# Rotary halves as separate chunks, four heads' scores in four 32-row groups, and ranked first loads

## The chip, the cores and the metric

One Trainium2 chip; the kernel runs on one of its cores. The metric is the device time of one execution in microseconds (us), the median of several runs. Engines are named as the profile names them: PE (TensorE matmul), PEld (its weight loads), DVE (VectorE), ACT (ScalarE), POOL (GpSimd), SP (SyncE, which issues most DMAs here).

## The reference

Two layers over a sequence of 256 tokens with 1024 channels, all float32. A layer first projects x to 7168 columns: a convolution branch (1024), differential attention q, k, v (512 each), a second attention q, k, v (512 each; its blocks are 256 keys long, so at this length it is plain causal attention), and 3072 gate columns. Both attentions rotate q and k before the scores; a head has 64 dimensions, and its first 32 are paired with its last 32:

```python
def apply_rope(x, cos, sin):
    x1, x2 = jnp.split(x, 2, axis=-1)
    return x * c + jnp.concatenate([-x2, x1], axis=-1) * s
```

so the rotated first half is x1·cos − x2·sin and the second x2·cos + x1·sin. Scores are q·k over the 64 dimensions, masked, softmaxed, and multiplied with v. The convolution branch is a causal depthwise convolution of 31 taps over 512 channels, then a LayerNorm. The three branches are projected, gated, summed and projected again (LayerNorm), and a squared-ReLU MLP with 4096 hidden units follows (LayerNorm).

## The kernel before

**Precision.** Every large weight and activation is split into a rounded part ("hi", by ACT) and the rest ("lo", by DVE), and a product is three matmuls (`mm3`, line 392). A weight tile is 512 KB: a DMA into one of 4 `raw` buffers, an ACT cast to `whi`, a DVE subtraction to `wlo` (`Weights.get`, line 342; 8 buffers each). Scores, the transposed probabilities and the transposes are plain fp32 matmuls, which the profile shows as two passes each.

**Order.** No instruction is issued where it is written. All are recorded in a plan (class `Plan`, line 42), and `order` (line 235) then builds one fixed list per engine: it walks forward in a clock of its own, and whenever an engine is free gives it the ready operation with the earliest latest-start time (`late`, line 181). For this clock it books a price for each operation (lines 131 to 147): for PE 0.422 ns a column with a floor of 108 ns, for a plain fp32 matmul 1.69 ns a column (so 433 ns for 256 columns and 216 ns for 128); for DVE 1.042 ns an element and 68 ns, 62 more with a per-partition scalar. The plan knows nothing of matmuls that run side by side in different rows of the array. On the chip the lists stay as they are: an engine that is early waits at its next list entry. PSUM is 8 banks in three pools, `pm` 2, `pa` 4 and `pt` 2 (line 30).

**Head.** x transposed comes in five pieces over SP, between the first weights (lines 448 to 457). The convolution's input projection of layer 0 runs over output half b, then over the eight 128-row slices kt, then over the two token tiles t (line 601), so all of x and the first four weights are needed before the second four. Weight tile i of the eight holds slices 2(i mod 4) and 2(i mod 4)+1 of output half i//4.

**Attention.** After the v projections come eight units of 128 columns x 2 (q and k of two attentions, two halves each; `qkunit`, line 566), two weights each; after each weight `tick` (line 579) runs the attention steps that are due. A unit's two column chunks are two pairs of heads, with 64 partitions to a head. `rope` (line 639) moves the halves of each head past each other by four ACT copies of 32 partitions, then multiplies twice and adds on DVE. `attn_scores` (line 657) does one pair of heads: four matmuls with 64 contraction rows, two `pa` banks. The further steps of a pair (transpose, times v, normalise, transpose back) use `pa` too and are due three ticks apart; pairs start at ticks 7, 9, 11, 14, 16, 18, 20 and 22 (line 777). Ticks 1 to 16 are the q and k weights, 17 to 24 the first gates.

**Gates.** `tunit` (line 545) makes 256 gate columns in two halves of 8 + 8 matmuls, the first half in a `pm` bank, the second in a `pt` bank; `tsum` (line 561) empties each bank by one ACT and one DVE instruction. It also serves the MLP.

**Convolution taps.** 124 DVE instructions a layer (`tap`, line 589) that only the LayerNorm in the last gates needs. They are ready all the time, so the planner fills every free moment of DVE with them.

Of the kernel before, what the change touches and what calls it, by code (L numbers as in the profile page):

```python
# [9 lines left out]
F32 = mybir.dt.float32  # L10
# [31 lines left out]
class Plan:  # L42
# [11 lines left out]
    class Op:  # L54
        __slots__ = ("i", "eng", "cost", "fn", "deps", "succ", "tiles", "late", "start", "end",
                     "bytes", "left", "ready", "bias")

# [9 lines left out]
    def __init__(self, nc):  # L67
        self.nc = nc
        self.ops = []
        self.tiles = {}  # L70
        self.tags = {}
        self.bias = 0.0
        for k, e in (("PE", nc.tensor), ("Activation", nc.scalar), ("DVE", nc.vector),
                     ("Pool", nc.gpsimd), ("SP", nc.sync)):
            setattr(self, k, Plan.Engine(self, e, k))
# [34 lines left out]
    def record(self, name, fn, method, args, kw):  # L110
# [10 lines left out]
        op.bytes = 0  # L121
        op.bias = self.bias
        op.fn = lambda: fn(*args, **kw)  # L123
        main = outs[-1] if "out" not in kw else kw["out"]
# [110 lines left out]
    def order(self):  # L235
        ops = self.ops
        self.latest()
        for op in ops:
            op.late += op.bias
            op.left = len(op.deps)  # L240
            op.ready = 0.0
            op.start = None
# [89 lines left out]
class Weights:  # L332
# [8 lines left out]

    def get(self, **dims):
        plan, i = self.plan, self.i
        self.i += 1
        raw = plan.tile(self.pool, [P, 1024], F32, "raw", RAWS)
        hi = plan.tile(self.pool, [P, 1024], F32R, "whi", NW)
        lo = plan.tile(self.pool, [P, 1024], F32R, "wlo", NW)
        n = 512 if i < 3 else 1024
        for c in range(0, 1024, n):
            s = slice(c, c + n)  # L350
            plan.SP.dma_start(raw[:, s], self.order[i][:, s])
            plan.Activation.copy(hi[:, s], raw[:, s])
            plan.DVE.tensor_sub(lo[:, s], raw[:, s], hi[:, s].bitcast(F32))
        pat = "p (" + " ".join(list(dims) + ["n"]) + ") -> p " + " ".join(list(dims) + ["n"])
        return [a.rearrange(pat, **dims) for a in (hi, lo)]
# [3 lines left out]
def kernel(ctx: ExitStack, tc: tile.TileContext, x, xT, w_in, w_p2, w_o, w_f1, w_f2,  # L359
# [52 lines left out]
    for l in range(L):  # L412
        order += [w_in[l, i] for i in range(32)]
        for step, b in GATED:
            if step == "gate":
                order += [w_in[l, 32 + 8 * b + i] for i in range(8)]
            else:
                order += [w_p2[l, 4 * b + i] for i in range(4)]
        order += [w_o[l, i] for i in range(8)]
        f1 = [w_f1[l, i] for i in range(32)]  # L420
        f2 = [w_f2[l, i] for i in range(32)]
        order += f1[:6]
        for i in range(6, 32, 2):
            order += f2[i - 6:i - 4] + f1[i:i + 2]
        order += f2[26:]
# [22 lines left out]
    X = x_new()  # L448
    for h in range(2):
        a = slot(F32, "xt32")  # L450
        for c0, c1 in ((0, 256), (256, 512), (512, 1024)) if h == 0 else ((0, 512), (512, 1024)):
            s = slice(c0, c1)
            k = (4 * h + c0 // 256) % 2
            n = (c1 - c0) // 256
            R.SP.dma_start(a[:, s], xT[:, h * 1024 + c0:h * 1024 + c1])
            split(*[v[:, k:k + n] for v in x_pair(X, 2 * h + c0 // 512)],
                  a[:, s].rearrange("p (k n) -> p k n", k=n))
    cst_t = R.tile(const, [P, 896], F32, "cst", 1)
# [62 lines left out]
    for l in range(L):  # L521
# [22 lines left out]

        def tunit(ticks=True):
            out = []
            for c in range(2):
                w = W.get(k=KT)
                ps = bank(("pm", "pt")[c])
                hi, lo = w  # L550
                for kt in range(KT):
                    R.PE.matmul(ps, hi[:, kt], x_both(X, kt), start=kt == 0, stop=False)
                for kt in range(KT):
                    R.PE.matmul(ps[:, 0:SEQ], lo[:, kt], x_at(X, kt)[0], start=False,
                                stop=kt == KT - 1)
                out.append(ps)
                if ticks:
                    tick()
            return out
# [38 lines left out]

        wc = [W.get(k=2) for _ in range(8)]
        pp = [[bank("pa"), bank("pm")] for _ in range(NT)]  # L600
        seq = [(t, b, kt) for b in range(2) for kt in range(KT) for t in range(NT)]
        if l:
            seq.sort(key=lambda e: e[0])
        for t, b, kt in seq:
# [32 lines left out]


        def rope(ps, dst):
            qq = R.tile(work, [P, 1024], F32, "zz", 3)  # L640
            q, qr = qq[:, :512], qq[:, 512:]
            for a in range(0, P, 64):
                R.Activation.copy(qr[a:a + 32], ps[a + 32:a + 64])
                R.Activation.copy(qr[a + 32:a + 64], ps[a:a + 32])
            p3 = ps.rearrange("p (c n) -> p c n", c=2)
            q3 = q.rearrange("p (c n) -> p c n", c=2)
            qr3 = qr.rearrange("p (c n) -> p c n", c=2)
            cb = cosT.rearrange("p (o n) -> p o n", o=1).broadcast_to([P, 2, SEQ])
            sb = sinT.rearrange("p (o n) -> p o n", o=1).broadcast_to([P, 2, SEQ])
            R.DVE.tensor_mul(q3, p3, cb)  # L650
            R.DVE.tensor_mul(qr3, qr3, sb)
            R.DVE.tensor_add(dst, q, qr)

        QK = {}
        o_sb = {}

        def attn_scores(b, pair):

            q, k = [QK[b, w, pair // 2][:, pair % 2] for w in 'qk']
            pt = R.tile(work, [P, 2, 384], F32, "pt", 2)  # L660
            mn = col(4, "mn")
            ll = col(4, "ll")
            li = col(4, "li")
            for e in range(2):
                ps = bank("pa")
                r = slice(64 * e, 64 * e + 64)
                R.PE.matmul(ps[:, 0:256], q[r, 128:256], k[r], start=True, stop=True)
                R.PE.matmul(ps[:, 256:384], q[r, 0:128], k[r, 0:128], start=True, stop=True)
                for (s, m, j) in ((slice(0, 256), slice(0, 256), 2 * e),
                                  (slice(256, 384), slice(128, 256), 2 * e + 1)):  # L670
                    R.DVE.tensor_tensor_reduce(
                        out=pt[:, e, s], in0=ps[:, s], in1=maskq[:, m], scale=-0.125,
                        scalar=3.0e38, op0=ALU.add, op1=ALU.min, accum_out=mn[:, j:j + 1])
                    R.Activation.activation(pt[:, e, s], pt[:, e, s], AF.Exp, bias=mn[:, j:j + 1],
                                         scale=-1.0, accum_out=ll[:, j:j + 1])
            R.DVE.reciprocal(li, ll)
            return pt, ll, li

        def transp(src):

            ps = bank("pa")
            R.PE.transpose(ps[:, 0:128], src[:, 256:384], ident)
            R.PE.transpose(ps[:, 128:256], src[:, 0:128], ident)
            R.PE.transpose(ps[:, 256:384], src[:, 128:256], ident)
            return ps
# [10 lines left out]

        def d_a(h):
            pt, ll, li = attn_scores(0, h)
            cc = col(2, "cc")
# [16 lines left out]
        def d_c(h):  # L716
            t, li = state['d', h]
            ps = bank("pa")
            hs = slice(h * 128, (h + 1) * 128)
# [17 lines left out]
        def d_d(h):  # L737
            o = state['d', h]
            ps = bank("pa")
            R.PE.transpose(ps[:, 0:128], o[:, 128:256], ident)  # L740
# [3 lines left out]

        def m_a(j):
            pt, ll, li = attn_scores(1, j)
            for e in range(2):
# [13 lines left out]
        def m_c(j):  # L761
            t = state['m', j]
            t = t.rearrange("p (e n) -> p e n", e=2)
            ps = bank("pa")
            for k, (c0, c1) in enumerate(((0, 256), (256, 384))):
# [8 lines left out]

        jobs = [[lambda f=f, h=h: f(h) for f in (d_a, d_b, d_c, d_d)] for h in range(4)]
        jobs += [[lambda f=f, h=h: f(h) for f in (m_a, m_b, m_c)] for h in range(4)]
        start = [7, 9, 11, 14, 16, 18, 20, 22]
        ev = []
        for i, (j, s) in enumerate(zip(jobs, start)):
            for k, f in enumerate(j):  # L780
                ev.append((s + 3 * k, -k, i, f))
        for e in sorted(ev, key=lambda e: e[:3]):
# [185 lines left out]
        for i in range(3, 16):  # L968
            do2(i - 3)
            ps = tunit()  # L970
            hsplit(i, ps)
# [23 lines left out]
def _layout(x, w_in, b_gate, conv_w, conv_b, conv_ln_g, conv_ln_b, w_conv_out,  # L995
# [21 lines left out]
    for l in range(L):  # L1017
# [3 lines left out]
        for q, k in ((dq, dk), (mq, mk)):  # L1021
            a, b = tu(q), tu(k)
            u += [a[:2], b[:2], a[2:], b[2:]]
# [23 lines left out]
    cosT = np.concatenate([c, c, c, c])  # L1047
    sinT = np.concatenate([-s, s, -s, s])
    i = np.arange(P)
# [28 lines left out]
```

## Time and profile before

| what | value |
|---|---|
| time, median of 3 runs | 861.02 us (860.42 to 861.96) |
| the profiled execution: its own time | 865.14 us |
| the profiled execution: its span | 861.8 us |
| PE busy, share of the span | 843.6 us, 98% |
| DVE busy | 657.2 us, 76% |
| ACT busy | 544.7 us, 63% |
| DMA, mean over the span | 182 GB/s |

The span is from the first to the last instruction of the core. Matmuls are pipelined and the ends shown are modelled, so starts of matmuls are compared rather than ends. A group's idle time is that of its engine just before it, with what ended the wait.

### The profile page before, as it was taken

The numbers are of one execution on the slowest core, as the hardware profiler recorded it, in microseconds if no ns is written. First come the engines' busy times: TensorE is split into PE (matmuls) and PEld (weight loads), VectorE is DVE, ScalarE is ACT, GpSimd is POOL, SyncE is SP. The second block draws the span as 40 slices with busy tenths as digits, with TensorE's granted clock in tenths as the row PEclk, the third lists the DMA queues.
The fourth block names the chain that finished last, engine by engine and source line by source line (L and its number), as shares of the span: only waits on it lengthen the run. The fifth ranks groups of instructions, "written<-read, shape, count | busy, mean of one in ns | idle before, by whom it ended". The sixth has DMA issues, their size and how long they took to land.

```text
span 861.8 us, 13202 instructions
## 1 busy us (share of the span) xinstructions
PE 843.6 (98%) x4938; PEld 738.3 (86%) x4938; DVE 657.2 (76%) x1124; ACT 544.7 (63%) x917; POOL 18.1 (2%) x26
## 2 busy tenths in 40 slices
PE   7999989999999999999999999999999999999996
PEld 5889978889988888888888999888898888888885
DVE  5789999997876755555688999999787876555545
ACT  6558899567437666666354789975562586666650
POOL 0000000000000000000000001000000000000000
PEclk9999999999999999999999999999999999999999
DMA  8865433556536856655355853355644577665511
GB/s 314 296 206 175 146 104 123 173 189 200 168 144 226 302 191 192 195 195 194 100 176 180 269 157 124 98 175 175 211 144 152 185 282 241 196 195 188 186 66 49
DMA packets 44559, 156.95 MB, mean 182 GB/s; under 512 B 4944, under 2 KB 5712, under 8 KB 44496
## 3 DMA queue, kind: packets, MB, share of 16 engines
q1 hardware_dynamic: 44496, 156.13, 54.7%
q8 instruction: 38, 0.62, 0.3%
q14 instruction: 25, 0.20, 0.1%
HBM read 155.06 MB, written 1.05 MB: 181 GB/s over the span
## 4 chain that ended last, share of the span: by engine, by line
PE 88%; DVE 4%; ACT 3%; DMA 3%; issue 1%; SPq 1%; POOL 0%; DVEq 0%; ACTq 0%
PE pm L123 42%; PE pa L123 30%; PE pt L123 16%; DMA raw<-in_w_f_dram 2%; DVE wlo L123 1%; DVE big L123 1%; ACT zz L123 1%; DMA big<-in_xT_dram 1%; ACT pt L123 1%; ACT o L123 1%; SPq L123 1%; ACT whi L123 0%; ACT big L123 0%; DVE pt L123 0%; DVE col L123 0%
## 5 line engine op out<-in xcount | busy, mean ns | idle before, releaser
L123 DVE TENSOR_TENSOR wlo<-raw,whi 128x1024 fp32r<-128x1024 f32 (+1 forms) x283 | 341.2, 1211 | 143.4 <-ACT whi L123 141.8
L123 ACT CAST whi<-raw 128x1024 fp32r<-128x1024 f32 (+1 forms) x283 | 293.7, 1044 | 184.9 <-PE pm L123 62.7
L123 PE MATMUL pm<-big,whi 128*128 128x256 f32 (+1 forms) x1296 | 270.2, 320 | 0.1
L123 PEld LDWEIGHTS pm<-big,whi 128*128 128x128 f32 x1296 | 215.4, 191 | 17.6 <-DVE big L123 0.7
L123 PE MATMUL pa<-whi,big 128*128 128x512 f32 x704 | 219.2, 393 | 3.4 <-ACT big L123 2.1
L123 PE MATMUL pm<-big,wlo 128*128 128x256 f32 x848 | 182.4, 282 | 0.0
L123 PEld LDWEIGHTS pa<-whi,big 128*128 128x128 f32 x704 | 130.4, 189 | 30.7 <-ACT big L123 2.5
L123 PEld LDWEIGHTS pm<-big,wlo 128*128 128x128 f32 x848 | 140.4, 191 | 4.0
L123 PE MATMUL pa<-wlo,big 128*128 128x512 f32 x352 | 137.4, 392 | 0.0
L123 DVE SCALAR_TENSOR_TENSOR big<-hpad,half,big 128x256 f32<-128x256 f32 x240 | 103.5, 478 | 0.0
L123 PE MATMUL pt<-big,whi 128*128 128x512 f32 x400 | 101.1, 394 | 0.0
L123 PE MATMUL pm<-whi,big 128*128 128x512 f32 (+1 forms) x320 | 91.7, 371 | 0.0
L123 PEld LDWEIGHTS pt<-big,whi 128*128 128x128 f32 x400 | 71.9, 189 | 12.8
L123 PEld LDWEIGHTS pa<-wlo,big 128*128 128x128 f32 x352 | 66.5, 189 | 14.0
L123 PEld LDWEIGHTS pm<-whi,big 128*128 128x128 f32 x320 | 57.9, 188 | 10.3 <-ACT zz L123 0.4
L123 PE MATMUL pm<-wlo,big 128*128 128x512 f32 (+1 forms) x160 | 59.1, 370 | 0.0
L123 PEld LDWEIGHTS pt<-big,wlo 128*128 128x128 f32 x400 | 54.6, 190 | 3.9
L123 ACT ACTIVATE zz<-zz 128x512 f32<-128x512 f32 x58 | 36.8, 634 | 32.5 <-DVE zz L123 32.4
L123 PE MATMUL pt<-big,wlo 128*128 128x256 f32 x400 | 55.8, 282 | 0.0
L123 ACT COPY zz<-pm 32x512 f32<-32x512 f32 (+1 forms) x72 | 40.8, 567 | 8.9 <-DVE zz L123 6.1
L123 ACT ACTIVATE pt<-pt,col 128x256 f32<-128x256 f32 (+1 forms) x96 | 40.8, 457 | 1.3 <-DVE col L123 1.1
L123 PEld LDWEIGHTS pm<-wlo,big 128*128 128x128 f32 x160 | 30.1, 188 | 4.9
(89 smaller groups left out, 571.5 us busy)
## 6 DMA issues: line engine op xcount, KB each, us to landing
raw<-in_w_f_dram SPq DMA_DIRECT2D x128, 512.0 KB, 3.5
raw<-in_w_in_dram SPq DMA_DIRECT2D x109, 512.0 KB, 3.8
raw<-in_w_p_dram SPq DMA_DIRECT2D x24, 512.0 KB, 3.4
raw<-in_w_o_dram SPq DMA_DIRECT2D x16, 512.0 KB, 4.0
big<-in_rows_dram SPq DMA_DIRECT2D x10, 512.0 KB, 6.1
raw<-in_w_in_dram SPq DMA_DIRECT2D x6, 256.0 KB, 5.9
big<-in_x_dram SPq DMA_DIRECT2D x2, 512.0 KB, 7.1
out_dram<-big SPq DMA_DIRECT2D x4, 256.0 KB, 2.0
```

The costliest lines, as they stand in the source:

```text
L123: op.fn = lambda: fn(*args, **kw)
```

## The change

(1) The host reorders the q and k columns so that a unit's first chunk holds the first rotary halves of four heads (32 partitions a head) and its second chunk the second halves. `rope` needs no ACT copies then: DVE multiplies the unit by cos, multiplies each chunk, read from PSUM in the other's place, by sin, and subtracts or adds chunk by chunk. (2) `attn_scores` does four heads at once: 16 matmuls with 32 contraction rows, in four row groups of the array, into all four `pa` banks; each head's score is the sum over the two chunks. Calls are due at ticks 7, 12, 18 and 24. All later attention steps use the two `pt` banks, and the gates' `tunit` therefore both `pm` banks (the MLP's keeps `pm` and `pt`). (3) In layer 0 the first loads have a rank that goes before every other priority, the first two pieces of x are issued by ACT, and the convolution's projection takes the weights of both output halves for two slices of x before it goes on.

```diff
         for op in ops:
             op.late += op.bias
+            if op.rank is not None:
+                op.late = op.rank - 1e9
...
-        order += [w_in[l, i] for i in range(32)]
+        order += [w_in[l, i] for i in ([0, 4, 1, 5, 2, 6, 3, 7] if l == 0 else range(8))]
+        order += [w_in[l, i] for i in range(8, 32)]
...
+    xt32 = [R.tile(work, [P, 1024], F32, "zz", 3) for _ in range(2)]
+    pieces = ((0, 0), (256, 0.5), (512, 1.5), (1024, 3.5), (1536, 5.5), (2048, None))
+    for (c0, rank), (c1, _) in zip(pieces, pieces[1:]):
+        R.rank = rank
+        (R.Activation if c0 < 1024 else R.SP).dma_start(
+            xt32[c0 // 1024][:, c0 % 1024:c0 % 1024 + c1 - c0], xT[:, c0:c1])
+        R.rank = None
...
-        def tunit(ticks=True):
+        def tunit(tags=("pm", "pm")):
...
-                ps = bank(("pm", "pt")[c])
+                ps = bank(tags[c])
...
+            seq = [(t, b, 2 * j + k) for j in range(KT // 2) for b in range(2) for k in range(2)
+                   for t in range(NT)]
...
-            for a in range(0, P, 64):
-                R.Activation.copy(qr[a:a + 32], ps[a + 32:a + 64])
-                R.Activation.copy(qr[a + 32:a + 64], ps[a:a + 32])
...
             R.DVE.tensor_mul(q3, p3, cb)
-            R.DVE.tensor_mul(qr3, qr3, sb)
-            R.DVE.tensor_add(dst, q, qr)
+            for c in range(2):
+                R.DVE.tensor_mul(qr3[:, c], p3[:, 1 - c], sinT)
+            R.DVE.tensor_sub(d3[:, 0], q3[:, 0], qr3[:, 0])
+            R.DVE.tensor_add(d3[:, 1], q3[:, 1], qr3[:, 1])
...
+        def attn_scores(b, u):
+            q, k = [QK[b, w, u] for w in 'qk']
+            ps = [bank("pa") for _ in range(4)]
+            for cols, qs, ks in ((slice(0, 256), slice(128, 256), slice(0, 256)),
+                                 (slice(256, 384), slice(0, 128), slice(0, 128))):
+                for c in range(2):
+                    for e in range(4):
+                        r = slice(32 * e, 32 * e + 32)
+                        R.PE.matmul(ps[e][:, cols], q[r, c, qs], k[r, c, ks], start=c == 0,
+                                    stop=c == 1, tile_position=(32 * e, 0))
...
-            ps = bank("pa")
+            ps = bank("pt")
...
-        start = [7, 9, 11, 14, 16, 18, 20, 22]
+        for b, u, t in ((0, 0, 7), (0, 1, 12), (1, 0, 18), (1, 1, 24)):
...
-            ps = tunit()
+            ps = tunit(("pm", "pt"))
...
-            a, b = tu(q), tu(k)
+            a, b = [tu(v.reshape(D, 2, 4, 2, 32).transpose(0, 1, 3, 2, 4).reshape(D, 512))
+                    for v in (q, k)]
```

## Rows read from the trace of the kernel before

**Rows 1.** The page, part 1: busy time, share of the span, instructions.

```profile
PE 843.6 (98%) x4938; PEld 738.3 (86%) x4938; DVE 657.2 (76%) x1124; ACT 544.7 (63%) x917; POOL 18.1 (2%) x26
```

**Rows 2.** Windows: length; busy PE, PEld, DVE, ACT, POOL; PE clock, DMA share, GB/s.

```profile
0.00:20.00 20.00, 15.38 (x50) 11.58 (x51) 11.29 (x17) 11.98 (x17) 0.40 (x5) 0.91 0.88 308
...
37.00:186.00 149.00, 146.47 (x1000) 132.23 (x1000) 139.72 (x313) 113.03 (x235) 4.03 (x4) 0.99 0.51 163
461.30:603.80 142.50, 140.98 (x981) 127.94 (x981) 137.25 (x308) 109.77 (x231) 4.23 (x4) 1.00 0.50 160
```

**Rows 3.** Windows, the taps' tile alone: length; busy DVE, ACT, POOL.

```profile
37.00:186.00 149.00, 52.74 (x124) 0.00 (x0) 0.00 (x0) 0.99 0.51 163
```

**Rows 4.** Timeline of PE, the head: start, length, what [idle before].

```profile
5.12 1.27 PE L123 MATMUL pa<-whi,big 128*128 128x512 f32 x4
...
7.83 0.39 PE L123 MATMUL pa<-wlo,big 128*128 128x512 f32 x1
9.55 1.19 PE L123 MATMUL pa<-whi,big 128*128 128x512 f32 x4 [1.33 <-ACT whi L123]
...
14.67 1.52 PE L123 MATMUL pa<-whi,big 128*128 128x512 f32 x3 [2.10 <-ACT big L123]
...
33.07 0.73 PE L123 MATMUL pm<-whi,big 128*128 128x512 f32 x2
```

**Rows 5.** Timeline of ACT, the head.

```profile
5.72 0.62 ACT L123 CAST whi<-raw 128x512 fp32r<-128x512 f32 x1 [0.67 <-DMA raw<-in_w_in_dram]
8.15 0.62 ACT L123 CAST big<-big 128x512 fp32r<-128x512 f32 x1 [1.81 <-DMA big<-in_xT_dram]
8.88 2.64 ACT L123 CAST whi<-raw 128x512 fp32r<-128x512 f32 x4
```

**Rows 6.** Timeline of SP, the head: one issue.

```profile
1.17 0.42 SPq L123 DMA_DIRECT2D raw<-in_w_in_dram  x1
```

**Rows 7.** Groups by form: busy us, mean ns | idle before.

```profile
L123 ACT COPY zz<-pm 32x512 f32<-32x512 f32 x64 | 37.0, 578 | 7.0 <-DVE zz L123 6.1
...
L123 DVE TENSOR_TENSOR zz<-pm,cst 128x512 f32<-128x512 f32 x16 | 10.9, 682 | 0.0
...
L123 DVE TENSOR_TENSOR zz<-zz,pm 128x256 f32<-128x256 f32 x26 | 10.8, 415 | 1.2 <-ACT zz L123 1.2
```

**Rows 8.** Timeline of PE: the scores of one pair of heads, and the next.

```profile
101.02 0.93 PE L123 MATMUL pa<-qk,qk 64*128 64x256 f32 x8
101.88 0.39 PE L123 MATMUL pm<-big,whi 128*128 128x256 f32 x1
```

**Rows 9.** Waits of PE, 60 to 190 us: total, times, longest.

```profile
PE pa L123 <- ACT o L123: 2.5, 2, 1.9
```

**Rows 10.** Timeline, gates of layer 0, after the longest of these waits.

```profile
121.80 3.33 PE L123 MATMUL pm<-big,whi 128*128 128x512 f32 x8
```

**Rows 11.** Timeline of all engines, one half of a gate unit in layer 1.

```profile
583.98 2.00 PE L123 MATMUL pt<-big,whi 128*128 128x512 f32 x8
...
584.50 1.22 DVE L123 TENSOR_TENSOR wlo<-raw,whi 128x1024 fp32r<-128x1024 f32 x1
...
585.64 0.41 DVE L123 TENSOR_TENSOR big<-big,pm 128x256 f32<-128x256 f32 x1
585.82 1.12 PE L123 MATMUL pt<-big,wlo 128*128 128x256 f32 x8
585.97 1.27 DVE L123 SCALAR_TENSOR_TENSOR big<-hpad,half,big 128x256 f32<-128x256 f32 x3
...
586.77 2.00 PE L123 MATMUL pm<-big,whi 128*128 128x512 f32 x8
...
587.16 1.22 DVE L123 TENSOR_TENSOR wlo<-raw,whi 128x1024 fp32r<-128x1024 f32 x1
```

**Rows 12.** Chain of waits in order of time: one weight of a q or k unit.

```profile
94.36 2.87 PE pm L123 x24
```

More of the change, by code (lines that the diff above doesn't have):

```diff
@@ L55 @@
         __slots__ = ("i", "eng", "cost", "fn", "deps", "succ", "tiles", "late", "start", "end",
-                     "bytes", "left", "ready", "bias")
+                     "bytes", "left", "ready", "bias", "rank")
     class Engine:
@@ L72, in __init__ @@
         self.bias = 0.0
+        self.rank = None
         for k, e in (("PE", nc.tensor), ("Activation", nc.scalar), ("DVE", nc.vector),
@@ L122, in record @@
         op.bias = self.bias
+        op.rank = self.rank if method == "dma_start" else None
         op.fn = lambda: fn(*args, **kw)
@@ L340, in __init__, with get @@
         self.i = 0
-    def get(self, **dims):
+    def get(self, rank=None, **dims):
         plan, i = self.plan, self.i
@@ L347, in get @@
         lo = plan.tile(self.pool, [P, 1024], F32R, "wlo", NW)
-        n = 512 if i < 3 else 1024
+        n = 512 if i < 2 else 1024
         for c in range(0, 1024, n):
             s = slice(c, c + n)
+            plan.rank = rank
             plan.SP.dma_start(raw[:, s], self.order[i][:, s])
+            plan.rank = None
             plan.Activation.copy(hi[:, s], raw[:, s])
@@ L448 @@
     X = x_new()
[L449 to L457, printed above, removed]
+    xt32 = [R.tile(work, [P, 1024], F32, "zz", 3) for _ in range(2)]
[5 more added lines that the diff above has]
+        R.rank = None
+    for (c0, _), (c1, _) in zip(pieces, pieces[1:]):
+        k, n = c0 // 256 % 2, (c1 - c0) // 256
+        split(*[v[:, k:k + n] for v in x_pair(X, c0 // 512)],
+              xt32[c0 // 1024][:, c0 % 1024:c0 % 1024 + c1 - c0].rearrange(
+                  "p (k n) -> p k n", k=n))
     cst_t = R.tile(const, [P, 896], F32, "cst", 1)
@@ L556, in tunit @@
                 out.append(ps)
-                if ticks:
-                    tick()
+                tick()
             return out
@@ L597, in tap @@
                                                op0=ALU.mult, op1=ALU.add)
-        wc = [W.get(k=2) for _ in range(8)]
+        fetch = [0, 4, 1, 5, 2, 6, 3, 7] if l == 0 else range(8)
+        wc = {}
+        for n, i in enumerate(fetch):
+            wc[i] = W.get(rank=n if l == 0 else None, k=2)
         pp = [[bank("pa"), bank("pm")] for _ in range(NT)]
-        seq = [(t, b, kt) for b in range(2) for kt in range(KT) for t in range(NT)]
-        if l:
-            seq.sort(key=lambda e: e[0])
+        if l == 0:
+            seq = [(t, b, 2 * j + k) for j in range(KT // 2) for b in range(2) for k in range(2)
+                   for t in range(NT)]
+        else:
+            seq = [(t, b, kt) for t in range(NT) for b in range(2) for kt in range(KT)]
         for t, b, kt in seq:
@@ L647, in rope @@
             qr3 = qr.rearrange("p (c n) -> p c n", c=2)
+            d3 = dst.rearrange("p (c n) -> p c n", c=2)
             cb = cosT.rearrange("p (o n) -> p o n", o=1).broadcast_to([P, 2, SEQ])
-            sb = sinT.rearrange("p (o n) -> p o n", o=1).broadcast_to([P, 2, SEQ])
             R.DVE.tensor_mul(q3, p3, cb)
-            R.DVE.tensor_mul(qr3, qr3, sb)
-            R.DVE.tensor_add(dst, q, qr)
+            for c in range(2):
+                R.DVE.tensor_mul(qr3[:, c], p3[:, 1 - c], sinT)
@@ L654 @@
+            R.DVE.tensor_sub(d3[:, 0], q3[:, 0], qr3[:, 0])
+            R.DVE.tensor_add(d3[:, 1], q3[:, 1], qr3[:, 1])
         QK = {}
         o_sb = {}
[L657 to L664, printed above, removed]
-                ps = bank("pa")
[L666 to L677, printed above, removed]
@@ new lines, in attn_scores @@
+        def attn_scores(b, u):
[8 more added lines that the diff above has]
+                                    stop=c == 1, tile_position=(32 * e, 0))
+            res = []
+            for i in range(2):
+                pt = R.tile(work, [P, 2, 384], F32, "pr", 2)
+                mn = col(4, "mn")
+                ll = col(4, "ll")
+                li = col(4, "li")
+                for e in range(2):
+                    for (s, m, j) in ((slice(0, 256), slice(0, 256), 2 * e),
+                                      (slice(256, 384), slice(128, 256), 2 * e + 1)):
+                        R.DVE.tensor_tensor_reduce(
+                            out=pt[:, e, s], in0=ps[2 * i + e][:, s], in1=maskq[:, m],
+                            scale=-0.125, scalar=3.0e38, op0=ALU.add, op1=ALU.min,
+                            accum_out=mn[:, j:j + 1])
+                        R.Activation.activation(pt[:, e, s], pt[:, e, s], AF.Exp,
+                                             bias=mn[:, j:j + 1], scale=-1.0,
+                                             accum_out=ll[:, j:j + 1])
+                R.DVE.reciprocal(li, ll)
+                res.append((pt, ll, li))
+            return res
@@ L679, in transp @@
         def transp(src):
-            ps = bank("pa")
+            ps = bank("pt")
             R.PE.transpose(ps[:, 0:128], src[:, 256:384], ident)
@@ L695, in branch, with d_a @@
             return BR[b]
-        def d_a(h):
-            pt, ll, li = attn_scores(0, h)
+        def d_a(h, sc):
+            pt, ll, li = sc
             cc = col(2, "cc")
@@ L717, in d_c @@
             t, li = state['d', h]
-            ps = bank("pa")
+            ps = bank("pt")
             hs = slice(h * 128, (h + 1) * 128)
@@ L738, in d_d @@
             o = state['d', h]
-            ps = bank("pa")
+            ps = bank("pt")
             R.PE.transpose(ps[:, 0:128], o[:, 128:256], ident)
@@ L742, in d_d, with m_a @@
             split(*at(branch(0), ALLP, h), ps[:, 0:256], subg)
-        def m_a(j):
-            pt, ll, li = attn_scores(1, j)
+        def m_a(j, sc):
+            pt, ll, li = sc
             for e in range(2):
@@ L763, in m_c @@
             t = t.rearrange("p (e n) -> p e n", e=2)
-            ps = bank("pa")
+            ps = bank("pt")
             for k, (c0, c1) in enumerate(((0, 256), (256, 384))):
@@ L773, in m_c, with scores @@
                 split(*at(branch(1), r, j), ps[r, e * 256:(e + 1) * 256])
-        jobs = [[lambda f=f, h=h: f(h) for f in (d_a, d_b, d_c, d_d)] for h in range(4)]
-        jobs += [[lambda f=f, h=h: f(h) for f in (m_a, m_b, m_c)] for h in range(4)]
-        start = [7, 9, 11, 14, 16, 18, 20, 22]
+        def scores(b, u):
+            for i, sc in enumerate(attn_scores(b, u)):
+                (d_a, m_a)[b](2 * u + i, sc)
         ev = []
-        for i, (j, s) in enumerate(zip(jobs, start)):
-            for k, f in enumerate(j):
-                ev.append((s + 3 * k, -k, i, f))
+        for b, u, t in ((0, 0, 7), (0, 1, 12), (1, 0, 18), (1, 1, 24)):
+            ev.append((t, 0, 2 * b + u, lambda b=b, u=u: scores(b, u)))
+            for i in range(2):
+                for k, f in enumerate(((d_b, d_c, d_d), (m_b, m_c))[b]):
+                    ev.append((t + i + 3 * (k + 1), -k, 2 * b + u,
+                               lambda f=f, h=2 * u + i: f(h)))
         for e in sorted(ev, key=lambda e: e[:3]):
@@ L1047, in _layout @@
     cosT = np.concatenate([c, c, c, c])
-    sinT = np.concatenate([-s, s, -s, s])
+    sinT = np.concatenate([s, s, s, s])
     i = np.arange(P)
```

## The prediction

> **What bounds the kernel now.** I read the page's first part first: PE is busy 98% of the span [rows 1], so time can only come from places where PE idles or runs slow, or from matmuls that take less. Next the timeline of PE, to find those places. The first is the head: matmuls start at 5.12 us, stop before 9.55 and before 14.67, and the projection gives way to the v projections at 33.07 [rows 4]. The second and third are the two stretches of attention and gates, which I bound by the first and the last convolution tap, 37 to 186 us in layer 0 and 461.3 to 603.8 us in layer 1. PE idles 149.00 - 146.47 = 2.5 us in the one and 142.50 - 140.98 = 1.5 us in the other [rows 2]. In layer 0 the idle time is two waits for ACT to free a `pa` bank [rows 9], and the eight matmuls after the longer one take 3.33 us [rows 10] where eight of the same form take 2.00 [rows 11], another 1.3 us of slow clock. The reader is to see one more thing in the windows: DVE is busy 139.72 of 149 us and 137.25 of 142.5 us there [rows 2], and 52.74 us of that are 124 taps [rows 3]. The taps are filler, but on the chip they stand in DVE's list between instructions that PE waits for. DVE is as full as PE, and its order is fixed.
>
> **The head.** The projection is 96 matmuls; eight take 585.82 - 583.98 = 1.84 us [rows 11], so 96 take 22.1 us. From 5.12 to 33.07 it is 27.95 [rows 4]: 5.9 us are lost. The new order asks for x and the weights of both halves at the rate at which they are used. I take the landings as the ACT casts that waited for them show them, by bytes: 768 KB (two pieces of x, one weight) by 5.72, 256 KB more by 8.15, and then 256 KB every 0.66 us from 8.88 on, four casts in 2.64 us [rows 5]. In the new order the weight of the other half lands by 8.15 and 8.88, the third piece of x by 9.5, the next weight by 10.9. The twelve matmuls of the first weight end about 8.06 as now, one matmul after 7.83 [rows 4]. The next twelve start when the first half of their weight is cast, 8.15 + 0.62 = 8.77 [rows 5], and end at 11.5. The next weight is cast whole (1.24 us at most, two halves of 0.62; I take 1.1), so PE goes on at 12.0. From there each weight feeds twelve matmuls, 2.76 us, and lands in 1.3 us, so nothing stops it: 72 more take 16.6 us, to 28.6. I take a gain of 4.3 us of the 5.9; the ends are 0 (the early slow rate, 256 KB in 2.4 us, holds on) and 5.9. That x now starts on ACT costs nothing: two issues of 0.42 us [rows 6] lie in the time in which ACT waits for the first piece; without that cover it would be 0.8 us. That this weight no longer comes in halves (`n = 512 if i < 2`) is in the sum, as that cast.
>
> DMA engines are busy 0.88 of the first 20 us at 308 GB/s [rows 2], so order, not a second queue, is what I count. The Trainium skill, DMA: Bandwidth & Descriptors, Issuing engines are not separate DMA queues, says that loads issued from different engines share the same 16 DMA engines, so spreading them saves issue time alone. By it the second queue is worth at most two issues; if the row's rate were a limit of one queue, up to the whole 5.9 us could come back.
>
> **Rotary.** Per unit four ACT copies of 578 ns go, 2.3 us, 16 units: 37.0 us of ACT [rows 7]. PE idles in layer 0 because ACT is late there, so I count all of that back: 2.5 + 1.3 = 3.8 us, and the 1.5 us of layer 1. Ends: 0 and 5.3. On DVE three instructions of 512 columns (0.68 us) become one of 512 and four of 256 (0.415) [rows 7]: 2.34 instead of 2.05, +0.3 us a unit at most, 2.3 us a layer, hidden only as long as DVE is not what PE waits for; the plan books most of it, so it displaces taps. Not counted by itself.
>
> **Scores on PE.** A pair of heads takes 101.88 - 101.02 = 0.86 us [rows 8]; eight pairs a layer, 6.9 us. Its two 64-row groups run side by side: two heads' passes in the time of one. A call of four heads has twice the passes per group, so if four groups run side by side it takes between 1.5 and 1.72 us, I take 1.6: four calls 6.4, a gain of 0.5 us a layer. If only two groups do, 3.4 us a call; if none, 5.3 or more. The row with two groups is nearest to four. TensorEngine Tiling (Array Packing), Overview, in the Trainium skill gives up to 4 times for contraction dims of 32, and TensorE: Matmul & The Clock Gate, Measured speedup vs the span model, gives 3.07 measured; by that a call would be some 1.7 us, an estimate from that page, 0.1 us from mine.
>
> **What the planner makes of it.** This is the term that decides the sign. The planner books a call one matmul after another: 8 x 433 + 8 x 216 ns = 5.2 us (line 136), where a pair was booked at 1.3. For the 3.6 us that PE will not need, it gives DVE taps to do, and these stand in DVE's list before whatever PE wants next. Before, the error was 1.30 - 0.86 = 0.44 a pair, 3.5 us a layer; now 4 x 3.6 = 14.4 us. PE comes early by that much, less what it loses elsewhere against its booking: a q or k weight is booked at 24 x 0.108 = 2.59 us and takes 2.87 [rows 12], 16 x 0.28 = 4.5; a half of a gate unit is booked at 2.59 and takes 586.77 - 583.98 = 2.79, 8 x 0.20 = 1.6 up to the last call [rows 11]; some 0.8 for v. DVE keeps to its booking: the lo of a weight is booked at 1.135 us and the next instruction starts 1.14 later, three taps are booked at 1.19 and take 587.16 - 585.97 = 1.19 [rows 11]; I allow DVE up to 2% more, some 2 us by the last call. Net, PE is early by 14.4 - 6.9 = 7.5 to 9.5 us a layer. Before the same sum is 3.5 - 6.9, below zero, and indeed no wait for DVE of this kind stands in the rows.
>
> How early may PE be before it waits? Until now a gate half had two banks in each of two pools, two units of room. Now both halves use `pm`, and a bank is wanted again 2.79 us after it was full. It is emptied at 586.05 for a half that PE left at 583.98, 2.1 us [rows 11], and a transfer of the semaphore comes on top; the quickest such release I can build from these rows, 0.47 on ACT and 0.41 on DVE, gives about 1 us. So the room is 0.5 to 1.8 us, I take 1.2. What is queued behind is all of PE: it works its list in order. The stall is 7.5 to 9.5 less 1.2; I take 7.5 a layer. Ends: 0 (DVE's list has idle places that I don't see) and 10.
>
> **Sum**, against the profiled span of 861.8 us: -4.3 (head) - 3.8 - 1.5 (waits for ACT) - 1.0 (scores) + 15.0 (waits for DVE) = +4.4 us. The profiled execution itself took 865.14 us, 4.1 above the median of 861.02; the difference is laid on the median: 865.4 us.
>
> **Rivals.** (a) PE sets the pace: the lists leave DVE enough room, or the gates' releases stand early enough, and only the gains remain: -10.6 us, 850.4. For it: before, only ACT held PE up, and ACT loses 37 us. Against it: DVE has only 9.3 and 5.3 us free in the two stretches [rows 2]. Chance 0.28. (b) The wait for DVE is half of what I say, because the calls early in the q and k units are made good before the gates: -10.6 + 7.5 = -3.1, 857.9. Chance 0.15, a third of it within 0.2%. (c) The row groups don't run side by side: a call takes 5.3 us, the booking is right, PE is never early, and it pays 8 x 3.6 = 29 us itself: -9.6 + 29 = +19, 880. The pair's overlap [rows 8] speaks against it: 0.04. (d) The head gains nothing because the early rate of 256 KB in 2.4 us lasts, or the four `raw` buffers hold the order back: +8.7, 869.7. Chance 0.08. My forecast, PE held by DVE's list: 0.45, by itself 861 to 870.
>
> **Chances.** About 0.2% (1.7 us) can be told from no change. Faster: (a) 0.28, two thirds of (b) 0.10: 0.38. Within: a third of (b) 0.05 and the low edge of the forecast 0.05: 0.10. Slower: 0.52. The range leaves out half of (a), (c) and little else: 850 to 874.
>
> **What would show it.** Head: PE's first v matmul near 28.7 instead of 33.07; if it stands at 32 or later, step one is wrong. Scores: the 32 passes of a call within 1.5 to 1.8 us, eight starts close together; 3 us or more is rival (c). ACT: no wait of scores for `o` in the two stretches. The planner's step: waits of PE for DVE in the gates (a gate matmul in `pm` released by a DVE add), 5 us or more a layer, and DVE with less than 4 us idle between first and last tap. If PE's waits there are below 2 us a layer, the term of 15.0 is wrong and (a) holds.

## The result, and the profile after

The changed kernel takes 867.82 us (median of 4 runs, 866.51 to 868.89); the kernel before, run beside it on the same chip, takes 861.49 us (4 runs, 860.42 to 862.99). The ratio is 1.0071 with a 95% interval of 1.0049 to 1.0094: slower by 6.3 us. The forecast was 865.4 us, slower.

The page's first part of the changed kernel (columns as in [rows 1]), and below it its windows over the head and from the first to the last tap of each layer (columns as in [rows 2]):

```profile
PE 840.7 (97%) x5066; PEld 735.7 (85%) x5066; DVE 656.5 (76%) x1155; ACT 506.1 (58%) x852; POOL 16.2 (2%) x26
```

```profile
0.00:20.00 20.00, 18.47 (x73) 14.89 (x74) 12.53 (x21) 12.31 (x17) 0.40 (x5) 1.00 0.93 335
32.40:173.80 141.40, 134.00 (x1003) 120.50 (x1002) 138.23 (x326) 90.07 (x196) 3.14 (x4) 1.00 0.51 168
460.40:595.40 135.00, 128.04 (x965) 115.76 (x963) 130.94 (x317) 82.18 (x184) 3.14 (x4) 0.99 0.48 153
```

The reader is to see two opposite movements. In the head PE does 18.47 us of work in the first 20 where it did 15.38, and 73 matmuls instead of 50 [rows 2]. In the two stretches PE now idles 141.40 - 134.00 = 7.4 us and 135.00 - 128.04 = 7.0 us, where it idled 2.5 and 1.5 [rows 2], although ACT has lost 38.6 us of work. DVE idles 3.2 and 4.1 us.

The head and one call of scores, from the timeline of PE of the changed kernel:

```profile
5.77 1.20 PE L125 MATMUL pa<-whi,big 128*128 128x512 f32 x4 [0.34 <-ACT whi L125]
...
27.83 0.73 PE L125 MATMUL pm<-whi,big 128*128 128x512 f32 x2
...
70.91 1.59 PE L125 MATMUL pa<-qk,qk 32*128 32x256 f32 x32
72.43 0.39 PE L125 MATMUL pm<-big,whi 128*128 128x256 f32 x1
```

The first v matmul stands at 27.83 instead of 33.07 [rows 4]: 5.2 us earlier. PE starts 0.65 us later, and from 5.77 on it doesn't wait again in the head. A call of four heads takes 72.43 - 70.91 = 1.52 us.

So the 4.8 us between the spans (866.6 and 861.8) divide like this: -5.2 up to the first v matmul; from there to layer 1's first tap 460.40 - 27.83 = 432.6 us instead of 461.3 - 33.07 = 428.2, +4.4; from layer 1's first tap to the end 406.2 instead of 400.5, +5.7.

Last, where PE waits in layer 0 of the changed kernel, 32 to 175 us (total us, times, longest):

```profile
PE pm L125 <- DVE big L125: 2.4, 3, 0.9
PE pt L125 <- ACT o L125: 2.3, 1, 2.3
PE pt L125 <- ACT ptT L125: 1.1, 2, 0.9
PE pt L125 <- DVE am L125: 1.1, 1, 1.1
PE pm L125 <- DVE zz L125: 0.3, 1, 0.3
```

and the chain of waits of the changed kernel in order of time (start, us, what) up to the longest of them, the one for ACT's `o`, and then up to the longest for a DVE add in that layer:

```profile
98.97 0.74 DVE am L125 x2
99.71 1.14 DVE wlo L125
100.85 0.09 DVE col L125
100.94 0.37 DVE big L125
...
101.44 0.60 DVE zz L125
102.04 0.65 DVE am L125 x2
...
102.78 0.66 DVE zz L125 x2
...
104.73 0.63 ACT o L125 x2
105.36 0.04 issue
105.41 0.55 PE pt L125 x3
...
113.85 1.23 DVE wlo L125
...
115.49 1.18 DVE big L125 x3
116.67 0.07 DVE col L125
116.74 2.38 DVE big L125 x6
...
120.22 1.59 DVE big L125 x4
...
122.77 0.34 DVE big L125
```

In these chains `big` on DVE is a tap or the add that empties a gate's bank, and `pt`, `pm` and `pa` on PE name the bank that is written. The list of waits names ACT in the first case, but the chain of the changed kernel goes back through DVE's list one instruction after another; ACT's `o` is only its last link. In the second, thirteen taps (`big` x3, x6, x4) stand in DVE's list ahead of the add of 122.77, for which the gate matmul of 123.17 waits. In the kernel before, the chain stays on PE from 94.96 to 109.97 and then, up to the longest wait, runs mostly through ACT's list; its lines stand further down, with the account of the prediction.

### The profile page after: what moved, and what is told of

It reads as the page before. It is cut to its first block, busy times and chain, and to the rows that moved or that the text cites. A ratio compares the mean times of both kernels' runs of the same rounds, so it can differ in the third digit from the quotient of the medians.

```text
span 866.6 us, 13455 instructions
## 1 busy us (share of the span) xinstructions
PE 840.7 (97%) x5066; PEld 735.7 (85%) x5066; DVE 656.5 (76%) x1155; ACT 506.1 (58%) x852; POOL 16.2 (2%) x26
## 4 chain that ended last, share of the span: by engine, by line
PE 81%; DVE 13%; ACT 3%; DMA 1%; issue 1%; DVEq 0%; ACTq 0%
PE pm L125 42%; PE pa L125 29%; PE pt L125 10%; DVE big L125 6%; DVE wlo L125 3%; DVE pr L125 2%; DVE zz L125 1%; ACT whi L125 1%; ACT pr L125 1%; DMA raw<-in_w_in_dram 1%; DVE am L125 1%; DVE col L125 1%; DMA zz<-in_xT_dram 0%; ACT big L125 0%; DVE qk L125 0%
## 5 line engine op out<-in xcount | busy, mean ns | idle before, releaser
L125 PE MATMUL pm<-big,whi 128*128 128x256 f32 (+1 forms) x1488 | 320.2, 330 | 5.1 <-DVE big L125 4.5
L125 PEld LDWEIGHTS pm<-big,whi 128*128 128x128 f32 x1488 | 249.9, 191 | 29.2 <-DVE big L125 6.0
L125 PE MATMUL pm<-big,wlo 128*128 128x256 f32 x1040 | 209.6, 283 | 0.0
L125 PEld LDWEIGHTS pm<-big,wlo 128*128 128x128 f32 x1040 | 166.6, 191 | 5.7
L125 ACT ACTIVATE pr<-pr,col 128x256 f32<-128x256 f32 (+1 forms) x96 | 40.4, 447 | 30.8 <-DVE col L125 30.8
L125 PE MATMUL pt<-big,whi 128*128 128x512 f32 x208 | 52.4, 392 | 0.0
L125 PEld LDWEIGHTS pt<-big,whi 128*128 128x128 f32 x208 | 37.4, 189 | 6.6
L125 DVE TENSOR_TENSOR big<-zz,big 128x512 fp32r<-128x512 f32 (+1 forms) x37 | 25.0, 676 | 11.6 <-ACT big L125 11.6
L125 ACT CAST big<-pt 128x256 fp32r<-128x256 f32 (+1 forms) x40 | 13.4, 374 | 29.3 <-PE pt L125 28.7
L125 POOL TENSOR_TENSOR col<-col,mhalf 128x1 f32<-128x1 f32 (+1 forms) x20 | 15.6, 778 | 796.3 <-DVE col L125 796.3
```

## The experiments

Every ratio is to 7 runs of the kernel before, taken beside the experiment on the same chip. Their median was 863.5 us for the right price, the parts and the price of four times; 863.32 for the doubled price, the fewer taps, the banks with the doubled price and the second queue; 862.09 for the rest. Where two experiments with different medians are compared, the ratios are the safer guide. The theory on trial: PE is held because the planner books a call of scores (one run of `attn_scores`, four heads) at 5.2 us, gives the surplus, the booked time that PE doesn't need, to taps, and PE then meets DVE's list too early.

**The price alone, in the changed kernel.**

```diff
             op.cost = max(n * 1.69, 214) if wide else max(n * 0.422, 108)
+            if "tile_position" in kw:
+                op.cost /= 4
```

> The changed kernel with one thing different: the planner books a 32-row score matmul at a quarter of its price, so a call of four heads at 1.3 us instead of 5.2 (the trace of the changed kernel shows 1.5). Only the order of the lists changes. Theory 1 (the booking): PE's idle time in the two stretches between first and last tap, 7.4 and 7.0 us, falls below 3 us each, and the time by some 9 us, from 867.8 to 857 to 860. Theory 2 (the banks: two pt banks for all attention steps and one pm bank for each half of a gate are too few, whatever is booked): idle time and time stay, 866 to 869.

Measured: 850.62 us, ratio 0.9849 (0.9834 to 0.9863). The right price moves the changed kernel from slower to faster, by 17.2 us between the medians and by 19.2 when each is taken against the kernel before that ran beside it (+6.3 and -12.9). That is more than the 9 us that I expected. Only the price is changed, so it was what cost the time. The windows of this kernel from the first to past the last tap:

```profile
32.40:186.00 153.60, 153.59 (x1130) 140.05 (x1129) 145.98 (x336) 100.96 (x212) 3.34 (x5) 1.00 0.50 165
455.00:600.00 145.00, 144.99 (x1085) 132.61 (x1084) 137.32 (x322) 96.14 (x205) 3.94 (x4) 1.00 0.47 154
```

PE idles 0.01 us in each; DVE has 7.6 and 7.7 us free. This is the state of rival (a): PE sets the pace. That the time is that rival's 850.4 is partly chance, since the kernel before ran at 863.5 beside it: the gain is 12.9 us, where rival (a) had 10.6.

**The parts alone.** One kernel has part (3) of the change, the head; the other parts (1) and (2), rotary, scores and banks.

```diff
-        order += [w_in[l, i] for i in range(32)]
+        order += [w_in[l, i] for i in ([0, 4, 1, 5, 2, 6, 3, 7] if l == 0 else range(8))]
+        order += [w_in[l, i] for i in range(8, 32)]
```

> The kernel before with the head of the change alone: ranked first loads, the first pieces of x from ACT, the projection's order in layer 0. In the changed kernel the first v matmul came 5.2 us earlier (27.83 for 33.07). If the whole of it reaches the end: 856 us. If DVE's list or later loads eat a part: 857 to 860.

```diff
-            for a in range(0, P, 64):
-                R.Activation.copy(qr[a:a + 32], ps[a + 32:a + 64])
...
+                        R.PE.matmul(ps[e][:, cols], q[r, c, qs], k[r, c, ks], start=c == 0,
+                                    stop=c == 1, tile_position=(32 * e, 0))
```

> The kernel before with the rotary and score part of the change alone, the old head. If the two parts add up: 861.5 + 6.3 + 5.2 = 873 us, with 7 us idle on PE in each stretch. If the early head only brings DVE's list under pressure sooner: 868 to 870.

Measured: the head alone 854.75 us, ratio 0.9898 (0.9882 to 0.9915); rotary and scores alone 874.22, ratio 1.0120 (1.0103 to 1.0138). The head alone lies below both of my values; the other is near the 873 that I had for it from a head worth 5.2 us. So the loss is all in the attention part: PE idles there 7.7 us of the 149.00 and 7.1 of the 142.50 of [rows 2], as much as in the whole change. The parts don't add: -8.8 and +10.7 make +1.9, and the whole is +6.3. The head alone gains more than 5 us. Its first v matmul stands at 28.34, 4.7 us earlier, and PE's idle time in layer 0's stretch shrinks as well, to 146.00 - 145.42 = 0.6 us from 32 to 178, with a granted clock of 1.00 there instead of 0.99; in the whole change that stretch idles 7.4.

**The price alone, in the kernel before: too high by four and by two, and halved.** Four times puts a pair's surplus at some 4.3 us, twice at 1.7; half (0.65) lies a little below the 0.86 us that a pair takes [rows 8].

```diff
             op.cost = max(n * 1.69, 214) if wide else max(n * 0.422, 108)
+            if wide and ins[0].ap[0][1] == 64:
+                op.cost *= 4
```

> The kernel before with one thing different: the planner books the 64-row score matmuls at four times their price, so a pair at 5.2 us where the chip takes 0.86. Banks, rotary and matmuls are those of before. Theory 1: PE would be early by 8 x 4.3 = 35 us a layer, less 7 that it loses elsewhere, less the room of two gate units (5.6): it waits some 22 us a layer if the taps last that long, so 880 to 905 us. Theory 2: 860 to 863.

> The kernel before with the 64-row score matmuls booked at twice their price: 2.6 us a pair, 20.8 us a layer, the same booked total as in the changed kernel. Banks are those of before. PE would be early by 8 x (2.6 - 0.86) - 7 = 7 us a layer, and two banks a gate half leave it some 5.6 us of room: it waits about 1.5 us a layer more, 862 to 868 us. If the room is not what counts: as in the changed kernel 6 us a layer, 872 to 876.

> The kernel before, with the pairs' score matmuls booked at half their price, near what the trace shows (0.86 us a pair instead of 1.30). If PE's stall starts only where the booking of a layer runs ahead by more than PE loses elsewhere against it (the two kernels with pairs booked at two and four times lie on a line that meets no loss at about 3.7 us a layer of extra booking), the kernel before stands inside that allowance and gains nothing: 860 to 864. If every overbooked microsecond costs its share from zero on, 7 us less of booking gives 3 to 6 us: 857 to 860.

Measured: four times 907.92 us, ratio 1.0509 (1.0491 to 1.0528); twice 874.12, 1.0129 (1.0106 to 1.0152); half 854.50, 0.9920 (0.9901 to 0.9939). Divided by what each adds to or takes from the bookings of 16 pairs (62.4, 20.8 and 10.4 us), that is 0.71, 0.52 and 0.73 us of time for each booked one. Two of my expectations fell: that two gate units of banks give the kernel before room for a doubled price, and that it stands inside an allowance at its own. It was already losing to its price, by more than my other value for it too (3 to 6 us), and four times the price cost a little more than the 880 to 905 that I gave it.

Not all of that is idle time. Over their whole spans, 861.8 and 906.1 us, PE is busy 843.6 us in the kernel before and 861.0 with four times the price, for the same 4938 matmuls, and the mean granted clock is 0.994 and 0.983. So 17.4 of the 44.3 us are matmuls that took longer and 26.9 are idle time. And the list that PE meets isn't DVE's alone; the chain of the kernel with four times the price passes from taps (`big`) to copies of `rope` on ACT (`zz`):

```profile
103.36 1.98 DVE big L123 x5
...
105.89 1.19 DVE big L123 x3
...
109.95 0.57 ACT zz L123
...
110.54 0.58 ACT zz L123
```

The windows with the halved price, over the first stretch of [rows 2] and a slightly longer second:

```profile
37.00:186.00 149.00, 148.54 (x1030) 134.79 (x1029) 139.98 (x313) 114.32 (x239) 3.69 (x5) 1.00 0.50 161
455.00:603.80 148.80, 148.76 (x1029) 134.94 (x1028) 140.31 (x314) 114.03 (x237) 4.02 (x4) 1.00 0.48 155
```

PE idles 0.5 us instead of 2.5, and 0.04 instead of 1.5, with every ACT copy of `rope` still in place. Of the 9.6 us between the two spans, 1.5 are a quicker head of this one execution: the first v matmul stands at 31.60, and the granted clock of the first 20 us is 1.00 instead of 0.91.

**The taps as the medium.** The changed kernel with its wrong price, but 8 of the 31 taps; the other 23 are left out of the convolution.

```diff
-            for k in range(TAPS):
+            for k in range(8):
```

> The changed kernel, wrong price kept, with 8 of the 31 convolution taps (the convolution leaves out 23). Theory 1: the planner fills PE's booked but unneeded time with taps; with 32 instead of 124 of them a layer they run out before the score calls, DVE's list has idle places, DVE catches up, and PE's idle time of 7.4 and 7.0 us falls below 3: 855 to 861 us. Theory 2 (too few banks for PE's order): the waits are for banks, not for filler, and stay: 865 to 868.

Measured: 851.48 us, ratio 0.9866 (0.9845 to 0.9886). Without most of its filler the changed kernel runs like the one with the right price. But DVE is also emptier by 92 taps of some 0.4 us a layer, so this run shows that the stall needs the taps' work on DVE, not by itself that their place in the list is what matters; only the price runs speak for that. PE's waits of this kernel from 60 to 175 us:

```profile
PE pt L125 <- DVE am L125: 0.7, 1, 0.7
PE pt L125 <- ACT o L125: 0.7, 1, 0.7
PE pt L125 <- ACT ptT L125: 0.4, 1, 0.4
```

The waits that name ACT shrink with DVE's filler, though ACT has the same to do.

**The banks alone.** The pools of the changed kernel (gates in `pm` alone, later attention steps in `pt`) in the kernel before, with its pairs booked twice, and at their own price.

```diff
-                ps = bank(("pm", "pt")[c])
+                ps = bank(tags[c])
...
-            ps = bank("pa")
+            ps = bank("pt")
```

> As over2, and with the banks of the changed kernel: both gate halves in pm, all attention steps after the scores in pt (the probabilities' SBUF tile has a tag of its own). Same lead of 7 us a layer, but a room of only 1.2 us: PE waits 6 us a layer, 870 to 876 us. If the lead alone counts and not the room: equal to over2 within 2 us.

> The kernel before with the PSUM pools of the changed one (gates in pm alone, the later attention steps in pt) and nothing else. If the pools only take away room and cost nothing where PE isn't ahead of its booking: 861 to 865. If the later attention steps of two pairs in two banks hold PE up by themselves, the 8.7 us that they cost beside the doubled booking appear here too: 869 to 873.

Measured: 882.85 us, ratio 1.0232 (1.0203 to 1.0262), 8.7 us above the doubled price alone; and 867.62, ratio 1.0068 (1.0051 to 1.0085), 5.5 above the kernel before. The second lies between my two values, 861 to 865 for banks that cost nothing by themselves and 869 to 873 for banks that cost as much as beside the doubled price. The kernel's own price is too high as well, and with the right one the changed kernel has the same pools and PE idles 0.01 us. So the banks seem to cost as a part of the stall and not by themselves; the direct run, these pools in the kernel before with a right price, wasn't made.

**The second queue.** The kernel with the right price, its pieces of x issued by SP in the same ranks.

```diff
-        (R.Activation if c0 < 1024 else R.SP).dma_start(
+        R.SP.dma_start(
```

> The changed kernel with the score matmuls booked at a quarter (run book, 850.6 us) and the first three pieces of x on SP's queue with the same ranks instead of ACT's. If order is all and the queue nothing, as I predicted: the first v matmul stays within 0.7 us of 27.8 and the time within 1 us of book, 850 to 852. If the early landings of 256 KB in 2.4 us belong to one queue: first v matmul 29 to 31, 852 to 854.

Measured: 851.34 us, ratio 0.9864 (0.9842 to 0.9885), against 850.62 with two queues: no difference that these intervals show, and inside the 850 to 852 expected if order is all. The other sign I had named failed: in the traces the first v matmul comes 0.9 us later, at 29.04 instead of 28.15, at the edge of what I gave the rival of one slow queue (29 to 31).

**What the change is worth at the right price.** The head with halved pairs, and the changed kernel with a call booked at 2.6 us, between 5.2 and 1.3.

```diff
             op.cost = max(n * 1.69, 214) if wide else max(n * 0.422, 108)
+            if wide and ins[0].ap[0][1] == 64:
+                op.cost /= 2
```

> The head part of the change alone, with the pairs booked at half. This is the rival of the change with right prices (850.6): by the allowance, 853.5 to 855.5 as the head part alone, and then rotary and scores are worth some 4 us once they are booked right; if every overbooked microsecond costs, 849 to 852, and the rotary and score part is worth nothing even with right prices.

```diff
             op.cost = max(n * 1.69, 214) if wide else max(n * 0.422, 108)
+            if "tile_position" in kw:
+                op.cost /= 2
```

> The changed kernel with a call of four heads booked at 2.6 us (it takes 1.5) instead of 5.2 or 1.3. Between the two known times, 850.6 and 867.8: with an allowance of about 10 us over the program before the stall starts, 850.5 to 853; if the loss is in proportion to the booked surplus, a third of it, 855 to 858.

Measured: 852.57 us, ratio 0.9895 (0.9876 to 0.9914); and 849.09, ratio 0.9852 (0.9831 to 0.9872), the fastest median of all, within the interval of the price of a quarter. Taken one on top of the other, the halved price of the pairs gives 7.6 us, the head 1.9 more, and rotary and scores 3.5 more. So more than half of the whole gain of 13.0 us is the price. Both times lie outside my expectations, 853.5 to 855.5 or 849 to 852 for the first and 850.5 or more for the second. From a price of 5.2 us to 2.6 the time falls by 18.7 us between the medians, from 2.6 to 1.3 by none that shows: in proportion to the surplus it is not.

## Why the prediction was right, and where it was wrong

**The sign and the step that decides it** were right: in the changed kernel PE runs ahead of its booking and meets DVE's list. The price alone turns the change round (850.62), in the kernel before it makes the same loss (874.12, 907.92), and fewer taps take it away (851.48).

**The sum** gave +4.4 us for a measured 6.3. Its terms:

- Head, -4.3: -5.2 by the first v matmul. PE began later than I took it, but the weights came fast enough for it never to stop. Part of what came back is clock: in the kernel before, after its wait of 2.10 us [rows 4], PE ran at a granted clock of 0.66 from 15 to 20 us; now it has 1.00 there. Rival (d) is out. ACT issued three pieces of x, not the two that I counted; it had time for all three.
- Scores, 1.6 us a call: 1.52. Rival (c) is out. By the 3.07 times that the Trainium skill measured (TensorE: Matmul & The Clock Gate, Measured speedup vs the span model) I had estimated 1.7; the trace is 0.2 us better.
- Waits of PE in the stretches, net +9.7 (15.0 - 3.8 - 1.5): PE's idle time went from 4.0 to 14.4 us, +10.4, where 15.0 less the idle time counted back is 11.0; the other 1.3 us were slow clock. By stages, -0.5 for the scores included, I had +3.2 and +5.5 after the head; measured +4.4 and +5.7.

**What was wrong behind this net figure.** Two steps failed, and their errors largely cancel: the price cost the changed kernel 17 to 19 us where I had 15.0, and the kernel before 7.6 where I had counted 5.3 back, for another reason. The difference is 10 to 12 us where I had 9.7. That the sum came so close is in part luck.

First, "PE idles in layer 0 because ACT is late there, so I count all of that back". ACT was late, and four copies of `rope` (`zz`, 0.58 us each) stand in the chain of the kernel before up to the longest wait [rows 9], two of them among these lines:

```profile
114.89 0.57 ACT pt L123 x3
...
115.48 0.58 ACT zz L123
...
117.27 0.81 ACT o L123 x4
...
118.11 0.58 ACT zz L123
...
118.71 1.21 ACT pt L123 x3
...
119.93 0.64 ACT o L123 x2
...
120.61 1.26 PE pa L123 x4
```

But with the price halved and every copy kept, those waits are all but gone (0.5 us, and not for `o`). So the copies were not enough by themselves to make PE wait; PE met ACT's list too early, as it meets DVE's in the changed kernel. No run takes the copies away alone at the old price. My rows also left out layer 1, where 0.6 of the 1.5 us wait for DVE (`PE pa L123 <- DVE col L123: 0.6, 1, 0.6`), so "only ACT held PE up" was too much.

Second, the netting, "Before the same sum is 3.5 - 6.9, below zero, and indeed no wait for DVE of this kind stands in the rows". The kernel before lost 7.6 us to a surplus of 16 x 0.44 = 7.0, so what PE loses on weights elsewhere was no credit against it. A reading that fits, but that no run tests: where PE is late, DVE waits for it and starts level again, so that lateness isn't saved up for the scores later. Nor is the room, my 0.5 to 1.8 us, to be had by units of gates: with two units of it the kernel before still lost 10.8 us to the doubled price. That fewer banks cost time is so, 8.7 and 5.5 us, but no run measures the room itself.

**The sign in the trace that I named** held in half: waits for a DVE add in `pm` are 2.4 and 2.1 us a layer, not 5 or more. The rest are the attention's steps in `pt`, for ACT's `o` and `ptT` and for DVE's `am`, all without a call of scores waiting for `o` (no `pa` in the list), as I had said. That DVE idles under 4 us is so in layer 0 (3.2) and just not in layer 1 (4.1).

**The second queue** I held to be worth at most two issues, by the Trainium skill (DMA: Bandwidth & Descriptors, Issuing engines are not separate DMA queues). The two runs agree: 0.7 us between the medians, inside the intervals, and 0.9 at the first v matmul.

**Open** is why the changed kernel bears a surplus of 8 x (2.6 - 1.52) = 8.6 us at no cost, and the kernel before not its 7.0. Their pools, the number of calls and the ACT copies differ; no run changes these one by one. The price also enters the planner twice, in its clock and in the latest-start times, and no run separates the two. Open too is why the head, 5.2 us early, leaves only 1.9 between the medians of the two kernels with halved pairs; their traces show 3.8 at the first v matmul (the one without the new head is the execution with the quick clock) and 2.6 at the end.

## What to carry to other kernels

Where a planner writes fixed lists, make each price what the trace shows before judging a change of the work: a price too high by 0.44 us on 16 calls cost 7.6 us here, and one too high by 3.7 us on 8 turned a gain of 13 into a loss of 6. Work that runs side by side in the array was the wrong price here, and the surplus came back as waits for the lists of the other engines, above all where filler stood in them. Follow a wait's chain back to the list that holds it up; the engine named last may only be passing the delay on. And try the price before the cause that the chain suggests: in the kernel before the chain ended in real work on ACT, and still the price was enough to remove the wait.

## What the runs showed of the hardware

A pair of heads, 8 passes in two row groups, takes 0.86 us [rows 8]; a call of four heads, 32 passes in four row groups, takes 1.52 us. Four times the passes, of half the rows each, cost 1.8 times as much: the four groups run side by side too.

With x and weights asked for in the order of use, from two engines, the DMA share of the first 20 us rose from 0.88 to 0.93 and the rate from 308 to 335 GB/s [rows 2] (0.90 and 324 with the right price); with the same order on one engine it was 0.89 and 307 GB/s, and PE still did 67 matmuls in them instead of 50. The order, not the rate, fed PE.

A wait of PE can cost more than its idle time. After the wait of 1.91 us that ends at 120.61 in the kernel before, the granted clock was half of the full one for two microseconds; from 15 to 20 us, after the wait of 2.10 [rows 4], it was 0.66, and 16 matmuls fitted where the changed kernel, at 1.00, did 24 (lines: before, before, changed kernel; columns as in [rows 2]):

```profile
121.80:123.80 2.00, 2.00 (x6) 1.61 (x6) 2.00 (x11) 2.00 (x6) 0.00 (x0) 0.50 0.66 240
15.00:20.00 5.00, 5.00 (x16) 3.67 (x15) 3.88 (x5) 3.65 (x5) 0.00 (x0) 0.66 1.02 376
15.00:20.00 5.00, 5.00 (x24) 4.14 (x23) 3.53 (x8) 2.49 (x4) 0.00 (x0) 1.00 1.01 365
```

Not every wait did this: with the halved pairs the same wait in the head, 2.11 us, was followed by 1.00. These runs don't show what decides it.
